# Eight experts in a row: longer turns in the first product's loop, a loop in the second product, and the opening moved ahead of the hand-synchronised section

## The chip, the cores and the metric

One core of one Trainium2 chip. The time is the device time of one launch in microseconds (us); lower is better. The profile shows five engines, named as in its rows: PE (TensorE's matmuls, and PEld for its weight loads), DVE (VectorE), ACT (ScalarE), POOL (GpSimd) and SP (SyncE). An engine's sequencer reads its instructions in order; rows of instructions that the sequencer does alone (address arithmetic, branches, waits) carry a q behind the engine's name, as in PEldq.

## The reference

Eight experts, each with 256 tokens of 512 numbers; every expert has its own two weight matrices and biases.

```python
n_experts, capacity, hidden, expert_hidden = 8, 256, 512, 2048
h = np.matmul(x, w1) + b1[:, np.newaxis, :]
h = np.maximum(h, 0)
return (np.matmul(h, w2) + b2[:, np.newaxis, :]).astype(np.float32)
```

All inputs and the output are fp32 in HBM.

## The kernel before

**Tiling.** The weights, and x from expert 2 on, are turned into fp16 on their way by GpSimd's DMAs. x is transposed on VectorE in blocks of 32 by 32 (`transposes`, L166 to L187), so that the first product gives h transposed: 16 columns of 128 hidden units, each with 256 tokens, each the sum of four matmuls (L299) in one of four PSUM banks `ph`. ScalarE takes a column out of its bank, adds b1 and applies relu (L234) into `hT`. The second product takes, for each half of 128 tokens (`tb`), one matmul that lays b2 down as ones times b2 (L320) and 16 matmuls of 512 columns (L323), in two groups of eight (`lo` 0 and 8), since the last two experts' second weights come in two halves. VectorE evicts token half 0 and ScalarE token half 1 (`evict`, L189 to L203). The experts' outputs are stored in groups of four and two by GpSimd (`flush`), the last two singly by SyncE.

**Stages.** TensorE runs a loop of 11 stages (L288). In stage s it does the first product of expert s (if s is under 8) and then the second product of expert s - 3 (if s is at least 3; `LAG` is 3). So stages 0 to 2 hold a first product only, stages 3 to 7 both, stages 8 to 10 a second product only. The loop is a loop on the chip: its instructions stand once in the program, and addresses are worked out in registers by TensorE's sequencer ahead of each matmul. The first product is itself a loop on the chip (L295), four turns of four columns (`NPH` is 4). The second product is written out: 34 matmuls, one behind the other.

**What sets the order.** Everything after the two `tile_critical` lines (L88) is synchronised by hand with semaphores; the instructions of each engine run in the order written.

- POOL: the DMAs of w1, w2 and x in one queue (L144 to L154), with three buffers for each kind of weights. A load waits for the product that last used its buffer (L122, L130).
- SP: waits for each weight to land and then counts `s_go` up (`go`, L245); `s_go` is what TensorE waits for ahead of each first product (L293) and of each group of eight of the second (L315).
- PE: beside `s_go` it waits for the transposes (`s_xT`, L294), and for a free bank of `po` ahead of each token half (`s_free`, L319). A column waits until its `ph` bank is free: `s_credit` starts at 4, ScalarE adds one for each column taken out, each column's first matmul waits for its number in the turn (L307), and at the end of a turn 4 are taken off (L309).
- DVE: the opening (cast of x of expert 0, its transposes, cast of x of expert 1, transposes of b1), and then in each stage the transposes for the next expert and the eviction of half 0.
- ACT: 16 columns of a stage, then the eviction of half 1.

The opening (memset, a warming activation, b1's load, the two x loads, casts and transposes) stands inside the section, with semaphores of its own (`s_ones`, `s_self`, `s_b1`).

Of the kernel before, what the change touches and what calls it, by code (L numbers as in the profile page):

```python
# [10 lines left out]
def kernel(  # L11
# [12 lines left out]
    nc = tc.nc  # L24
# [4 lines left out]
    E, T, H = x.shape  # L29
# [44 lines left out]
    for first, n in GROUPS.items():  # L74
# [5 lines left out]
    po = ctx.enter_context(nc.psum_tensor("po", [P, 2 * nTB * H], fp32))  # L80

    s_last = sem("last_stores")
    nc.vector.sem_inc(s_last, 16 * len(HALVED))

    section = ctx.enter_context(ExitStack())
    section.enter_context(tc.tile_critical(  # L88
        sync_engine=mybir.EngineType.SP, no_gpsimd_drain=True))


    landed = {}

    def load(engine, key, **kw):
        landed[key] = sem(f"d_{key}")
        engine.dma_start(**kw).then_inc(landed[key], 16)  # L96

    s_ones = sem("ones")
    s_self = sem("dve_self")
    s_b1 = sem("b1T")  # L100
    s_xT = sem("xT")
    s_ph = sem("ph")
    s_credit = sem("ph_free")
    s_po = [sem(f"po{tb}") for tb in range(nTB)]
    s_free = [sem(f"po{tb}_free") for tb in range(nTB)]
    s_out = [sem(f"out{tb}") for tb in range(nTB)]
    s_go = sem("weights")


    for e in range(2):  # L110
        load(nc.sync, f"x{e}", out=x32[e][:], in_=x[e].rearrange("(p tb) h -> p tb h", tb=nTB))


    def load_x(first):
# [12 lines left out]

    def load_w2(e):
        if e >= NW:
            nc.gpsimd.wait_ge(s_po[1], e - NW + 1)  # L130
        dst = w2_sb[:, e % NW * nJ * H : (e % NW + 1) * nJ * H].rearrange("p (j h) -> p j h", j=nJ)
        src = w2[e].rearrange("(p j) h -> p j h", j=nJ)
        size = half if e in HALVED else nJ
        for lo in range(0, nJ, size):
            load(nc.gpsimd, f"w2_{e}_{lo}", out=dst[:, lo : lo + size], in_=src[:, lo : lo + size])
# [22 lines left out]


    nc.vector.sem_inc(s_last, -16 * len(HALVED))  # L160
    nc.vector.memset(ones1[:], 1.0).then_inc(s_ones, 1)  # L161
    nc.scalar.wait_ge(s_ones, 1)
    nc.scalar.activation(out=warm[:], in_=ones1[:], func=relu)  # L163
    load(nc.scalar, "b1", out=b1_rows[:], in_=b1.rearrange("e (b i) -> (e b) i", b=nB))

    def transposes(e):  # L166
        t, p0, R = x16[e]
        n = R // nTB
        if e >= 2:
            first = max(f for f in X_LOADS if f <= e)  # L170
            nc.vector.wait_ge(landed[f"x{first}"], 16)
            nc.vector.wait_ge(s_ph, nJ * (e - 1))
        mine = xT[:, e % 2 * nKC * T : (e % 2 + 1) * nKC * T].rearrange("p (kc t) -> p kc t", kc=nKC)
        last = None
        for g in range(T // R // B):
            src = t[p0 + B * g : p0 + B * (g + 1)]
            for b in range(nB):
                block = src[:, :, b * (H // nB) : (b + 1) * (H // nB)].rearrange(
                    "p (n tb) (i kc) -> p tb kc n i", tb=nTB, kc=nKC)
                dst = mine[b * B : (b + 1) * B].rearrange(  # L180
                    "p kc (tb g i n) -> p tb g kc n i", tb=nTB, i=B, n=n)
                if n == 1:
                    last = nc.vector.transpose(out=dst[:, :, g, :, 0, :], in_=block[:, :, :, 0, :])  # L183
                    continue
                for tb in range(nTB):
                    last = nc.vector.transpose(out=dst[:, tb, g], in_=block[:, tb])  # L186
        last.then_inc(s_xT, 1)  # L187

    def evict(e, tb):  # L189
        engine = nc.scalar if tb else nc.vector  # L190
        copy = nc.scalar.copy if tb else nc.vector.tensor_copy
        first, n = group_of.get(e, (e, 1))
        rows = P // n
        at = (e - first) * rows
        engine.wait_ge(s_po[tb], e + 1)
        for k in range(n):
            bank = (e % 2 * nTB + tb) * H
            last = copy(out=results[e][at : at + rows, k * nTB + tb, :],  # L198
                        in_=po[k * rows : (k + 1) * rows, bank : bank + H])
        last.then_inc(s_out[tb], 1)  # L200
        if e + 2 < E:
            engine.wait_ge(s_out[tb], e + 1)
            engine.sem_inc(s_free[tb], 1)  # L203

    for e in range(2):
        nc.vector.wait_ge(landed[f"x{e}"], 16)
        nc.vector.tensor_copy(out=x16[e][0][:], in_=x32[e][:]).then_inc(s_self, 1)  # L207
        nc.vector.wait_ge(s_self, e + 1)
        if e == 0:
            transposes(e)  # L210
    nc.vector.wait_ge(landed["b1"], 16)
    for b in range(nB):
        last = nc.vector.transpose(  # L213
            out=b1T[b * B : (b + 1) * B, nB - 1 - b : nB - 1 - b + nJ * B],
            in_=b1_rows[:].rearrange("r (i j) -> r j i", j=nJ),
        )
    last.then_inc(s_b1, 1)
    for s in range(E + LAG):
        if s + 1 < E:
            transposes(s + 1)  # L220
        if s >= LAG:
            evict(s - LAG, 0)

    nc.scalar.wait_ge(s_b1, 1)
    for s in range(E + LAG):
        if s < E:
            split = group_of.get(s, (s, 1))[1]
            if s > LAG:
                nc.scalar.wait_ge(s_po[1], s - LAG)
            for j in range(nJ):  # L230
                at = (s % (LAG + 1) * nJ + j) * T
                bias_at = j * B + s * nB + nB - 1
                nc.scalar.wait_ge(s_ph, nJ * s + j + 1)
                nc.scalar.activation(  # L234
                    out=hT[:, at : at + T].rearrange("p (tb k i) -> p tb k i", tb=nTB, k=split),
                    in_=ph[:, j % NPH, 0:T].rearrange("p (tb i k) -> p tb k i", tb=nTB, k=split),
                    func=relu,
                    bias=b1T[:, bias_at : bias_at + 1],
                    scale=1.0,
                ).then_inc(s_credit, 1)  # L240
        if s >= LAG:
            evict(s - LAG, 1)


    def go(key, n=1):  # L245
        nc.sync.wait_ge(landed[key], 16)
        nc.sync.sem_inc(s_go, n)
# [5 lines left out]
    for s in range(E + LAG):  # L253
        if s == 0:
            nc.sync.wait_ge(landed["b2"], 16)
        if s < E:
            go(f"w1_{s}")
        e = s - LAG
        if e >= 0 and e not in HALVED:
            go(f"w2_{e}_0", 2)  # L260
        elif e == E - 2:
            go(f"w2_{e}_0")
            go(f"w2_{e}_{half}")
        elif e == E - 1:
            go(f"w2_{e}_0")
            for tb in range(nTB):
                nc.sync.wait_ge(s_out[tb], e)
            store(E - 2, 0, P, nc.sync)
            go(f"w2_{e}_{half}")
# [5 lines left out]


    nc.tensor.sem_inc(s_credit, NPH)
    for tb in range(nTB):
        nc.tensor.sem_inc(s_free[tb], 2)
    nc.tensor.wait_ge(s_ones, 1)  # L280

    def take(s, n=1):
        nc.tensor.wait_ge(s, n).then_inc(s, -n)  # L283
# [4 lines left out]
    with nc.Fori(0, E + LAG, 1, engines=[PE]) as s:  # L288
        nc.tensor.wait_ge(s_credit, NPH)
        w_at = at(s % NW * (nKC * M), (NW - 1) * nKC * M)  # L290
        with nc.tensor.If(s < E):
            x_at = at((s & 1) * (nKC * T), nKC * T)
            take(s_go)  # L293
            take(s_xT)  # L294
            with nc.Fori(w_at, w_at + nJ, NPH, engines=[PE]) as w_from:  # L295
                w_from = w_from.with_bounds(min_val=0, max_val=(NW - 1) * nKC * M + nJ - NPH)
                for j in range(NPH):
                    for kc in range(nKC):
                        last = nc.tensor.matmul(  # L299
                            ph[:, j, 0:T],  # L300
                            w1_sb[:, bass.ds(w_from + (kc * M + j), P, nJ)],
                            xT[:, bass.ds(x_at + kc * T, T)],
                            start=(kc == 0),
                            stop=(kc == nKC - 1),
                        )
                        if kc == 0:
                            last.wait_op(s_credit, j + 1, "sem-ge")  # L307
                    last.then_inc(s_ph, 1)
                nc.tensor.sem_inc(s_credit, -NPH)  # L309
        with nc.tensor.If(s >= LAG):  # L310
            b_at = at((s - LAG) * H, (E - 1) * H)
            h_at = at(((s + 1) & LAG) * (nJ * T), LAG * nJ * T)
            p_at = at(((s + 1) & 1) * (nTB * H), nTB * H)
            for lo in range(0, nJ, half):
                take(s_go)  # L315
                for tb in range(nTB):
                    bank = po[:, bass.ds(p_at + tb * H, H)]
                    if lo == 0:
                        take(s_free[tb])  # L319
                        nc.tensor.matmul(bank, ones1[:], b2_sb[:, bass.ds(b_at, H)],  # L320
                                         start=True, stop=False)
                    for j in range(lo, lo + half):
                        last = nc.tensor.matmul(  # L323
                            bank,
                            hT[:, bass.ds(h_at + (j * T + tb * P), P)],
                            w2_sb[:, bass.ds(w_at + j * H, H)],
                            start=False,
                            stop=(j == nJ - 1),
                        )
                    if lo:  # L330
                        last.then_inc(s_po[tb], 1)

    section.close()
    nc.sync.wait_ge(s_last, 16 * len(HALVED))


# [28 lines left out]
```

## Time and profile before

| what | value |
|---|---|
| median of 3 runs | 184.51 us (184.13 to 184.54) |
| the profiled execution's own time | 184.6 us |
| its span, first to last instruction | 182.7 us |
| PE busy, matmuls | 137.7 us, 784 matmuls |
| DVE busy | 87.5 us |
| ACT busy | 72.8 us |
| read from HBM | 71.39 MB, 414 GB/s over the span |
| mean granted clock of TensorE | 0.981 of full speed |

How to read it: a timeline row holds the start and length in us, the engine, the line in the kernel, the operation, what it writes and reads, how many instructions the row joins, and in brackets the idle time of the engine ahead of it and what ended it. `PEq L283` means that TensorE's own sequencer, at a wait of L283, ended it. A group's row holds the busy time, the mean of one instruction in ns, and the idle time ahead of its instructions with its causes. A row of one line in a window holds the count, minimum, median and maximum in ns, and the start of the first and of the last in us. Matmuls are pipelined: each one's length is longer than the distance to the next.

### The profile page before, as it was taken

Reading aid. Unit: us, or ns where it says so; the run is one execution under the profiler, and the core shown is the slowest. Engines: PE = TensorE matmul, PEld = TensorE weight load, DVE = VectorE, ACT = ScalarE, POOL = GpSimd, SP = SyncE. Lnnn points to the kernel's source line nnn. Section 1 sums busy time; section 2 is a strip of 40 time slices with the busy share of each in tenths; the row PEclk is TensorE's granted clock in tenths of the full one; section 3 lists DMA queues with packets and bytes.
Section 4 is the critical chain, followed back from the end, with each engine's and each line's share of the span. In section 5 each row is a group of like instructions: output and inputs, shape, how many; then the busy total and the mean of one; then the engine's idle time right before and its main releaser. Section 6 shows DMA issues by size and latency. Waiting matters only on the chain. (4 is left out here: it accounts for less than half of the span.)

```text
span 182.7 us, 3079 instructions
## 1 busy us (share of the span) xinstructions
PE 137.7 (75%) x784; PEld 92.5 (51%) x784; DVE 87.5 (48%) x125; ACT 72.8 (40%) x152; POOL 12.5 (7%) x27
## 2 busy tenths in 40 slices
PE   0003886977958779777996779786996879999990
PEld 0003784865847654576355644585465834344340
DVE  0999938409300497998059931997060003030110
ACT  3001663774655740577019530775038610220101
POOL 6000003001020010100010000100020000301000
PEclk9999998898899999999999999999999999999999
DMA  5989998999999998999999999999899989999972
GB/s 192 278 179 228 230 226 183 222 230 228 212 196 219 237 215 190 230 226 222 194 219 226 230 208 197 230 226 222 187 226 226 230 185 219 213 217 231 423 294 115
DMA packets 3826, 40.46 MB, mean 221 GB/s; under 512 B 448, under 2 KB 464, under 8 KB 1136
## 3 DMA queue, kind: packets, MB, share of 16 engines
q0 software_dynamic: 3200, 38.28, 95.0%
q1 hardware_dynamic: 576, 2.10, 3.0%
q10 hardware_dynamic: 48, 0.07, 0.1%
q14 instruction: 2, 0.02, 0.0%
HBM read 71.39 MB, written 4.19 MB: 414 GB/s over the span
## 5 line engine op out<-in xcount | busy, mean ns | idle before, releaser
L299 PE MATMUL ph<-xT,w_sb 128*128 x512 | 75.7, 305 | 35.8 <-PEq L283 21.9
L299 PEld LDWEIGHTS ph<-xT,w_sb 128*128 x512 | 66.9, 146 | 45.0 <-issue 22.4
L234 ACT ACTIVATE hT<-ph,b1T 128x256 f16<-128x256 f32 x128 | 58.5, 475 | 42.9 <-PE ph L299 39.5
L186 DVE STREAM_TRANSPOSE xT<-x 32x256 f16<-32x256 f16 (+1 forms) x64 | 52.8, 893 | 25.9 <-DMA x<-in_x_dram 18.1
L323 PE MATMUL po<-w_sb,hT 128*128 x256 | 58.0, 380 | 0.1
L323 PEld LDWEIGHTS po<-w_sb,hT 128*128 x256 | 24.1, 97 | 30.2 <-issue 4.1
L198 DVE COPY out<-po 32x512 f32<-32x512 f32 (+1 forms) x20 | 13.7, 687 | 46.0 <-PE po L323 45.8
L198 ACT COPY out<-po 32x512 f32<-32x512 f32 (+1 forms) x20 | 11.6, 579 | 48.7 <-PE po L323 48.5
L96 POOL DMA_DIRECT2D w_sb<-in_w_dram x18 | 9.7, 544 | 144.9 <-PE po L323 74.8
L183 DVE STREAM_TRANSPOSE xT<-x 32x256 f16<-32x256 f16 x32 | 14.0, 436 | 0.5
L320 PE MATMUL po<-b_sb,ones 1*128 x16 | 6.1, 380 | 4.9 <-PEq L283 4.9
L198 DVE COPY x<-po 128x512 f32<-128x512 f32 x2 | 1.4, 692 | 13.4 <-PE po L323 13.4
L320 PEld LDWEIGHTS po<-b_sb,ones 1*128 1x128 f16 x16 | 1.4, 90 | 10.3 <-issue 10.3
L198 ACT COPY x<-po 128x512 f32<-128x512 f32 x2 | 1.2, 587 | 13.8 <-PE po L323 13.8
L213 DVE STREAM_TRANSPOSE b1T<-b_rows 32x512 f32<-32x512 f32 x4 | 4.1, 1024 | 0.1
L207 DVE CAST x<-x 128x1024 f16<-128x1024 f32 x2 | 1.4, 694 | 2.9 <-DMA x<-in_x_dram 2.9
L163 ACT ACT_TABLE_LOAD x1 | 1.3, 1283 | 0.9 <-SPq L88 0.9
L96 POOL DMA_DIRECT2D out_dram<-out x2 | 1.1, 542 | 7.7 <-ACT out L198 7.7
L96 POOL DMA_DIRECT2D x<-in_x_dram x2 | 1.1, 550 | 0.0
L161 DVE MEMSET ones<- 1x128 f16 x1 | 0.2, 165 | 1.2 <-SPq L88 1.2
L96 POOL DMA_DIRECT2D b_sb<-in_b_dram x1 | 0.5, 509 | 0.0
L163 ACT ACTIVATE warm<-ones 1x128 f16<-1x128 f16 x1 | 0.3, 308 | 0.0
(4 smaller groups left out, 0.4 us busy)
## 6 DMA issues: line engine op xcount, KB each, us to landing
w_sb<-in_w_dram POOLq DMA_DIRECT2D x14, 2048.0 KB, 35.7
w_sb<-in_w_dram POOLq DMA_DIRECT2D x4, 1024.0 KB, 16.1
out_dram<-out POOLq DMA_DIRECT2D x1, 2048.0 KB, 17.9
x<-in_x_dram SPq DMA_DIRECT2D x2, 512.0 KB, 5.1
x<-in_x_dram POOLq DMA_DIRECT2D x1, 1024.0 KB, 33.0
out_dram<-out POOLq DMA_DIRECT2D x1, 1024.0 KB, 13.1
out_dram<-x SPq DMA_DIRECT2D x2, 512.0 KB, 4.7
x<-in_x_dram POOLq DMA_DIRECT2D x1, 512.0 KB, 24.8
```

The lines of the kernel that those rows point to most:

```text
L96: engine.dma_start(**kw).then_inc(landed[key], 16)
L161: nc.vector.memset(ones1[:], 1.0).then_inc(s_ones, 1)
L163: nc.scalar.activation(out=warm[:], in_=ones1[:], func=relu)
L183: last = nc.vector.transpose(out=dst[:, :, g, :, 0, :], in_=block[:, :, :, 0, :])
L186: last = nc.vector.transpose(out=dst[:, tb, g], in_=block[:, tb])
L198: last = copy(out=results[e][at : at + rows, k * nTB + tb, :], in_=po[k * rows : (k + 1) * rows, bank : bank + H])
L207: nc.vector.tensor_copy(out=x16[e][0][:], in_=x32[e][:]).then_inc(s_self, 1)
L213: last = nc.vector.transpose(out=b1T[b * B : (b + 1) * B, nB - 1 - b : nB - 1 - b + nJ * B], in_=b1_rows[:].rearrange("r (i j) -> r j i", ...
L234: nc.scalar.activation(out=hT[:, at : at + T].rearrange("p (tb k i) -> p tb k i", tb=nTB, k=split), in_=ph[:, j % NPH, 0:T].rearrange("p ( ...
L299: last = nc.tensor.matmul(ph[:, j, 0:T], w1_sb[:, bass.ds(w_from + (kc * M + j), P, nJ)], xT[:, bass.ds(x_at + kc * T, T)], start=(kc == 0 ...
L320: nc.tensor.matmul(bank, ones1[:], b2_sb[:, bass.ds(b_at, H)], start=True, stop=False)
L323: last = nc.tensor.matmul(bank, hT[:, bass.ds(h_at + (j * T + tb * P), P)], w2_sb[:, bass.ds(w_at + j * H, H)], start=False, stop=(j == nJ ...
```

## The change

Four parts:

- **First product:** the inner loop makes two turns of eight columns instead of four of four. The four `ph` banks are used twice in a turn, so a column's number in the turn goes up to 8 and 8 credits are taken off at a turn's end.
- **Second product:** the two token halves are a loop on the chip of two turns, once for each group of eight matmuls, instead of being written out. The bank's offset is worked out from the loop's counter. One semaphore `s_po` counts both halves (2 e + tb + 1) instead of one for each.
- **Gating by SyncE:** TensorE no longer waits for the transposes nor for free `po` banks. SyncE waits for `s_xT` before it releases a w1, and from the third expert on for the evictions of the expert two back before it releases a w2.
- **Opening:** the memset, the warming activation, the loads of b1 and of x of experts 0 and 1, the casts, expert 0's transposes and those of b1 stand ahead of the section. The section's beginning waits, on PE, ACT, SP and DVE, until they are done; POOL's queue of loads stands ahead of that wait. The wait for the last stores is an instruction of SyncE behind the section.

```diff
-    for e in range(2):
-        load(nc.sync, f"x{e}", out=x32[e][:], in_=x[e].rearrange("(p tb) h -> p tb h", tb=nTB))
...
+    nc.vector.memset(ones1[:], 1.0)
+    tc.keep_in_program_order(nc.scalar.activation(out=warm[:], in_=ones1[:], func=relu))
+    tc.keep_in_program_order(nc.scalar.dma_start(
+        out=b1_rows[:], in_=b1.rearrange("e (b i) -> (e b) i", b=nB)))
+    for e in range(2):
+        nc.sync.dma_start(out=x32[e][:], in_=x[e].rearrange("(p tb) h -> p tb h", tb=nTB))
+    for e in range(2):
+        nc.vector.tensor_copy(out=x16[e][0][:], in_=x32[e][:])
+        if e == 0:
+            transposes(e)
+    for b in range(nB):
+        nc.vector.transpose(
+            out=b1T[b * B : (b + 1) * B, nB - 1 - b : nB - 1 - b + nJ * B],
+            in_=b1_rows[:].rearrange("r (i j) -> r j i", j=nJ),
+        )
+
+    section = ctx.enter_context(ExitStack())
+    by_hand = section.enter_context(tc.tile_critical(
+        sync_engine=mybir.EngineType.SP, no_gpsimd_drain=True))
...
+    nc.vector.sem_inc(s_xT, 1)
...
-        engine.wait_ge(s_po[tb], e + 1)
+        engine.wait_ge(s_po, nTB * e + tb + 1)
...
-        if e + 2 < E:
-            engine.wait_ge(s_out[tb], e + 1)
-            engine.sem_inc(s_free[tb], 1)
...
         if s < E:
+            nc.sync.wait_ge(s_xT, s + 1)
             go(f"w1_{s}")
         e = s - LAG
+        if e >= 2:
+            for tb in range(nTB):
+                nc.sync.wait_ge(s_out[tb], e - 1)
...
             take(s_go)
-            take(s_xT)
-            with nc.Fori(w_at, w_at + nJ, NPH, engines=[PE]) as w_from:
...
-                for j in range(NPH):
+            with nc.Fori(w_at, w_at + nJ, half, engines=[PE]) as w_from:
...
+                for j in range(half):
...
-                            ph[:, j, 0:T],
+                            ph[:, j % NPH, 0:T],
...
-                nc.tensor.sem_inc(s_credit, -NPH)
+                nc.tensor.sem_inc(s_credit, -half)
...
                 take(s_go)
-                for tb in range(nTB):
-                    bank = po[:, bass.ds(p_at + tb * H, H)]
+                with nc.Fori(h_at, h_at + T, P, engines=[PE]) as h_from:
+                    h_from = h_from.with_bounds(min_val=0, max_val=LAG * nJ * T + T - P)
+                    o_at = at(p_at + (h_from & P) * (H // P), (2 * nTB - 1) * H)
+                    bank = po[:, bass.ds(o_at, H)]
                     if lo == 0:
-                        take(s_free[tb])
...
-                            hT[:, bass.ds(h_at + (j * T + tb * P), P)],
+                            hT[:, bass.ds(h_from + j * T, P)],
...
-                        last.then_inc(s_po[tb], 1)
+                        last.then_inc(s_po, 1)
...
-    nc.sync.wait_ge(s_last, 16 * len(HALVED))
+    landing = nc.sync.nop().wait_op(s_last, 16 * len(HALVED), "sem-ge")
```

In the changed program a turn of the second product's first group holds, on TensorE's sequencer, a two-register step, three ALU steps (one a multiplication), two more steps, the bias matmul, eight pairs of a two-address step and a matmul, a two-register step and a branch; a turn of the second group has one step less ahead of its matmuls and no bias. In the kernel before, token half 1's matmuls each had a one-address step.

## The prediction

> **What bounds the kernel now.** I read the chain of work that ended last and the groups first, then the timeline of TensorE, then the waits of SyncE for the weights, and last the single lines of TensorE's sequencer.
>
> ```profile
> PE 17%; ACT 0%; issue 0%
> PE po L323 16%; PE po L320 1%; ACT x L198 0%
> ...
> L299 PE MATMUL ph<-xT,w_sb 128*128 x512 | 75.7, 305 | 35.8 <-PEq L283 21.9
> ...
> L323 PE MATMUL po<-w_sb,hT 128*128 x256 | 58.0, 380 | 0.1
> ```
>
> The chain is TensorE alone. The second product (L323) runs almost without a gap (0.1 us idle in 58.0). The first (L299) loses 35.8 us, 16.6 of it before its first matmul.
>
> ```profile
> 42.28 8.11 PE L299 MATMUL ph<-xT,w_sb 128*128 x48 [1.78 <-PEq L283]
> ...
> 55.04 2.35 PE L299 MATMUL ph<-xT,w_sb 128*128 x16 [1.74 <-PEq L283]
> ...
> 63.73 2.35 PE L299 MATMUL ph<-xT,w_sb 128*128 x16 [0.53 <-ACT hT L234]
> 67.06 0.37 PE L320 MATMUL po<-b_sb,ones 1*128 x1 [0.98 <-PEq L283]
> ...
> 74.79 1.91 PE L299 MATMUL ph<-xT,w_sb 128*128 x16
> 78.06 2.32 PE L299 MATMUL ph<-xT,w_sb 128*128 x16 [1.36 <-ACT hT L234]
> 80.92 2.36 PE L299 MATMUL ph<-xT,w_sb 128*128 x16 [0.54 <-ACT hT L234]
> 83.80 2.35 PE L299 MATMUL ph<-xT,w_sb 128*128 x16 [0.52 <-ACT hT L234]
> 87.13 0.37 PE L320 MATMUL po<-b_sb,ones 1*128 x1 [0.98 <-PEq L283]
> ...
> 135.00 1.91 PE L299 MATMUL ph<-xT,w_sb 128*128 x16
> ```
>
> Stages 4 to 7 repeat every 20.07 us (67.06 to 87.13). Stages without a second product take 12.76 us (42.28 to 55.04). After stage 7 only second products are left:
>
> ```profile
> 155.17 0.38 PE L320 MATMUL po<-b_sb,ones 1*128 x1
> ...
> 162.93 0.38 PE L320 MATMUL po<-b_sb,ones 1*128 x1
> ...
> 170.68 0.38 PE L320 MATMUL po<-b_sb,ones 1*128 x1
> ...
> 173.15 5.35 PE L323 MATMUL po<-w_sb,hT 128*128 x24
> ```
>
> They repeat every 7.76 us and end at 178.50. The weights arrive earlier. These rows are SyncE's releases, three windows of the one line:
>
> ```profile
> L247 SPq EVENT_SEMAPHORE  x5: 17/17/28, 15.7 to 57.2; - x5
> L247 SPq EVENT_SEMAPHORE  x7: 17/17/17, 71.8 to 129.9; - x7
> L247 SPq EVENT_SEMAPHORE  x5: 17/17/17, 139.6 to 163.8; - x5
> ```
>
> From 71.8 to 129.9 six steps bring three experts, 19.4 us each. The cover is 3.0 us at stage 4 (71.8 against 74.79), 5.1 at stage 7 (129.9 against 135.00) and 6.9 for the last expert's first half (163.8 against 170.68). So TensorE's stream is the bound, with the DMAs close behind.
>
> **What paces TensorE's stream.** The sequencer, lines of it in short windows (columns: count, min/median/max ns, first to last start):
>
> ```profile
> L309 PEldq EVENT_SEMAPHORE  x1: 51/51/51, 80.1 to 80.1; - x1
> L295 PEldq FUSED_REGOPS  x1: 42/42/42, 80.2 to 80.2; - x1
> L295 PEldq COMPARE_BRANCH  x1: 218/218/218, 80.3 to 80.3; - x1
> L295 PEldq MOVE  x1: 29/29/29, 80.6 to 80.6; - x1
> L299 PEldq ALU_OP  x1: 36/36/36, 80.7 to 80.7; - x1
> L299 PEldq FUSED_REGOPS  x2: 74/76/79, 80.8 to 80.9; - x2
> L295 PEldq COMPARE_BRANCH  x1: 83/83/83, 86.1 to 86.1; - x1
> L323 PEldq FUSED_REGOPS  x8: 74/74/79, 157.2 to 158.2; - x8
> L323 PEldq FUSED_REGOPS  x8: 46/46/51, 158.4 to 159.3; - x8
> L288 PEldq ALU_OP  x2: 36/36/36, 152.6 to 159.4; - x2
> L323 PEldq FUSED_REGOPS  x33: 46/57/98, 154.2 to 159.3; - x33
> ```
>
> Each matmul needs one address step. With two new addresses it takes 74 ns and the next follows after 0.155 us, with one 46 ns and 0.126 us (eight from 157.2 to 158.2, eight from 158.4 to 159.3). A turn's foot and head, the first five rows, take 0.7 us (80.1 to 80.8): the 0.52 to 0.54 us gaps above are the sequencer's, though the view names ACT. Their durations sum to 0.38, so each step costs its row plus about 0.06: ALU 0.095, move 0.09, a two-register step 0.10, a semaphore wait 0.11 to 0.15 (I take 0.15), a branch 0.275 taken (218) and 0.14 not taken (83). One pass over a last stage is 6.8 us (152.6 to 159.4), under TensorE's 7.76, so today the sequencer runs ahead there.
>
> **The change, part by part.**
>
> *Eight columns a turn.* Two of three turn ends go: 0.7 each, and four two-address steps become one-address ones (4 x 0.03): 0.83 each. Stages 0 to 3 gain 1.66. From stage 4 on the first boundary lies under a wait that stays:
>
> ```profile
> 74.99 2.35 ACT L198 COPY out<-po 32x512 f32<-32x512 f32 x4 [8.40 <-PE po L323]
> 77.53 2.34 ACT L234 ACTIVATE hT<-ph,b1T 128x256 f16<-128x256 f32 x6 [0.19 <-ACT out L198]
> ```
>
> ScalarE evicts the previous expert until 77.34, its first activation frees a bank near 78.0, and TensorE resumes at 78.06. So one boundary is gained there, 0.83. ScalarE keeps up: its backlog clears at 0.39 us a column (2.34 for 6) against 0.5 for four matmuls.
>
> *Second product as a loop over token halves.* Twice per expert a loop of two turns; weights' addresses are computed again in each, so all steps are two-address (0.155). A first-half turn: head of a two-register step, three ALU, two more steps and the bias matmul, 0.64; eight steps 1.24; 0.05 for the remainder of the stage number by three (98 against 57), now taken in every turn; foot 0.10 and a branch: 2.31 taken, 2.17 not. A second-half turn has one step less in its head and no bias: 2.18 and 2.05. With two waits for weights (0.30), two ALU, a step and a move (0.38) that is 9.4 us an expert. TensorE needs 1.94 a turn (7.76/4): now the sequencer is slower, and every turn shows. A pass in the tail adds 0.85 (ALU, move, two branches taken, one not): 10.25 instead of 7.76. Not shown before: the multiply as ALU step, nothing extra (36) up to the remainder step's 98, so 0 to 0.06 a turn; I take nothing, as ALU rows all read 36.
>
> The Trainium skill, "Advanced Engine Details and Errata", section "Control Flow Timing", gives about 108 ns for a compare-and-branch. The rows show 218 and 83. By the page's figure the 28 turns counted below would be about 1.2 us cheaper (an estimate), which would give 189.0; the rows decide.
>
> *Waits moved to SyncE.* TensorE's three waits a stage, for two free banks and the transposes, go; the sums here are without them. SyncE now waits for the transposes ahead of each first-product weight, and for evictions ahead of the second's; weights behind them in its queue wait too. The eviction asked for is two experts back, over at least one pass of 7.76 before the release is needed, so that pass hides it; if it came late, TensorE would stop by the lateness.
>
> *Opening outside the section.* TensorE, ScalarE and SyncE now enter behind all of VectorE's opening:
>
> ```profile
> 12.97 4.14 DVE L213 STREAM_TRANSPOSE b1T<-b_rows 32x512 f32<-32x512 f32 x4
> ...
> 62.07 9.96 DVE L186 STREAM_TRANSPOSE xT<-x 32x512 f16<-32x512 f16 x8 [14.64 <-DMA x<-in_x_dram]
> ...
> 16.62 5.31 PE L299 MATMUL ph<-xT,w_sb 128*128 x32 [16.62 <-PEq L283]
> ```
>
> It ends at 17.11; with VectorE's two semaphore steps (0.3) and the 0.9 from SyncE's release (15.7) to the first matmul (16.62), the first matmul comes at 18.3: 1.7 later. Bounds: 0.5 (17.11 itself) to 2.6 (one more such 0.9 hop). POOL's loads stand ahead of the wait and start as before.
>
> **The sum.** Stages 0 to 3 gain 6.6, lose 1.7: stage 3's first product ends 4.9 earlier, 66.1 (63.73 + 2.35) to 61.2. Then come 0.4 of loop end, a branch (0.14), 9.4, and 0.6 of ALU, move and branches to the wait for the next weights: 71.7, or 71.5 as the sequencer is 0.2 ahead of the last end. There something else is late: expert 4's transposes wait for x (landed at 62.07) and end at 72.03 whatever TensorE does. Through SyncE (0.9 as at the start, less a wait: 0.75) stage 4 starts at 72.8, 2.0 earlier than 74.79; 2.9 of the gain is lost. A period is then 64 matmuls 8.3 (8 x 0.155, 56 x 0.126), boundary 0.7, loop end and branch 0.5, second product 9.4, entry 1.1 (two ALU, two moves, two branches, a wait, a remainder step), and 0.1, as a measured turn (2.88, 80.92 to 83.80) is 0.05 over its steps: 20.1. TensorE's last matmul now trails the sequencer by 0.46, since its eight take 0.216 each ((5.35 - 0.38)/23) against 0.155; ScalarE's eviction, and so column 5, is later by that, 0.3 of it uncovered: add 0.3 from stage 5 on. Stage 5: 92.9; 6: 113.3; 7: 133.7 (135.00 before). Expert 5's bias matmul follows after 0.3 + 8.25 + 0.7 + 0.5 + 9.4 + 1.9 (0.85 and the head of a second product): 154.7 (155.17). Then 10.25 twice: 175.2 (170.68). To the last end it is 10.25 less that 1.9 and a foot, 8.1, and the trailing 0.46 and a matmul's 0.38: 184.1 instead of 178.5. That is 5.6 us more. Behind it stand the same eviction and store (the profiled run takes 184.6 us, span 182.7): 184.6 + 5.6 = **190.2**. The median of the runs is 184.51, 0.1 lower, so I keep 190.2. A measurement of this kernel can tell about 0.3% (0.55 us) from no change.
>
> **Rivals.**
>
> *Faster: the turn ends hide behind the matmuls*, as in the old tail. For: 58.0 us of L323 with 0.1 idle. Against: 0.7 at each L295 turn. If a turn costs no more than TensorE's 1.94, the DMAs bound next: stage 7 would start at 129.9 + 0.75 = 130.65, then 11.5 to expert 4's bias (12.34, 74.79 to 87.13, less 0.83) and four times 7.76: 173.2, or 179.3 in all. It decides below 2.0 us a turn: 5.6 us over the 28 turns of stages 4 to 10 is 0.2 off the mean 2.18. 8%.
>
> *Slower still: the halved clock.*
>
> ```profile
> 43.90:47.20 3.30, 3.17 (x16) 2.29 (x15) 3.25 (x9) 1.72 (x5) 0.00 (x0) 0.50 1.13 241
> ...
> 47.40:178.00 130.60, 111.91 (x630) 71.00 (x629) 55.27 (x55) 53.01 (x112) 6.89 (x13) 1.00 1.01 227
> ```
>
> The granted clock (third column from the end) was 0.50 from 43.9, behind the 1.78 us gap that ends at 42.28, and 1.00 after 47.4, though one gap of 1.74 (to 55.04) lies there. In the changed kernel the gap between the products grows from 0.98 to about 1.2, with smaller ones (0.35) after each turn. A half-clock stretch lets 16 matmuls of the first product through (the row's x16) instead of 27 (3.4/0.126), 1.4 us, of which about 1 stays lost after catching up; three of them: 193.2. 20%. The Trainium skill, "TensorE: Matmul & The Clock Gate", Part 1, lets the clock fall only after an idle window of about 3.4 us; by that rule it stays at 190.2, but the 0.50 above followed a shorter gap.
>
> *The early gain does not last to stage 4.* Its cover is short: 0.5 us between 71.5 and the release at 72.05. Entry at its upper bound (0.9 more) and two half-clock stretches of 1 us, which today's turn ends partly hide, put stage 4 at 72.8 + 2.4 = 75.2: 192.6. 12%.
>
> **The numbers.** Forecast 60% (187 to 193: 28 turns by 0.1 are 2.8 either way), faster rival 8%, clock 20%, lost gain 12%. The range 186.0 to 194.5 leaves out the faster rival and the ends of the others, together under 2 in 10. The faster rival's weight splits into 6% faster by over 0.3% and 2% within it; the forecast's low tail adds 1% within. Faster 0.06, same 0.03, slower 0.91.
>
> **What would show it.** First-product rows of 32 matmuls with one gap of 0.5 us between them. Stage 4's first matmul near 72.8, behind VectorE. Bias matmuls 10.2 us apart in the tail, with idle of about 0.35 us ahead of each turn put to the sequencer. The second product's group with several us idle instead of 0.1. Bias matmuls still 7.8 apart would prove the sum wrong, and a half clock after 75 us the second rival right.

## The result, and the profile after

The changed kernel takes **192.28 us** (median of 4 runs, 191.77 to 192.67), the kernel before 184.40 beside it: a ratio of 1.0427, 95% interval 1.0394 to 1.046. The forecast was 190.2 (range 186.0 to 194.5). The profiled run took 192.59, span 190.8.

The page of the changed kernel: the chain that ended last, by engine and by line, and two rows of the groups (busy time, mean ns | idle time before them).

```profile
PE 17%; issue 3%; ACT 2%; SPq 0%
PE po L314 16%; PE po L311 2%; ACT out L204 1%; ACT x L204 1%; SPq L241 0%; SPq L237 0%; SPq L261 0%
...
L314 PE MATMUL po<-w_sb,hT 128*128 x256 | 60.8, 380 | 5.8 <-issue 5.8
...
L311 PE MATMUL po<-b_sb,ones 1*128 x16 | 6.1, 382 | 13.4 <-issue 8.8
```

The chain is still TensorE, now with 3% of "issue", time in which it waits for nothing that the profile shows. The second product (L314) was idle for 0.1 us before and is for 5.8 now; its bias matmuls (L311) for 13.4. The timeline of TensorE shows where, in the first stages, in stage 4 and in the tail:

```profile
18.28 9.86 PE L289 MATMUL ph<-xT,w_sb 128*128 x64 [18.28 <-PEq L274]
29.78 4.40 PE L289 MATMUL ph<-xT,w_sb 128*128 x32 [1.64 <-PEq L274]
34.72 4.40 PE L289 MATMUL ph<-xT,w_sb 128*128 x32 [0.54 <-ACT hT L223]
...
51.72 9.50 PE L289 MATMUL ph<-xT,w_sb 128*128 x64 [1.63 <-PEq L274]
62.65 0.38 PE L311 MATMUL po<-b_sb,ones 1*128 x1 [1.43 <-issue]
...
72.53 4.44 PE L289 MATMUL ph<-xT,w_sb 128*128 x32 [0.73 <-PEq L274]
77.50 4.40 PE L289 MATMUL ph<-xT,w_sb 128*128 x32 [0.54 <-ACT hT L223]
83.31 0.38 PE L311 MATMUL po<-b_sb,ones 1*128 x1 [1.41 <-issue]
83.62 1.90 PE L314 MATMUL po<-w_sb,hT 128*128 x8
85.71 0.38 PE L311 MATMUL po<-b_sb,ones 1*128 x1 [0.19 <-issue]
86.03 1.90 PE L314 MATMUL po<-w_sb,hT 128*128 x8
88.31 1.90 PE L314 MATMUL po<-w_sb,hT 128*128 x8 [0.38 <-issue]
90.55 1.90 PE L314 MATMUL po<-w_sb,hT 128*128 x8 [0.35 <-issue]
93.17 4.46 PE L289 MATMUL ph<-xT,w_sb 128*128 x32 [0.72 <-PEq L274]
...
113.84 4.49 PE L289 MATMUL ph<-xT,w_sb 128*128 x32 [0.67 <-PEq L274]
...
156.09 0.38 PE L311 MATMUL po<-b_sb,ones 1*128 x1 [1.52 <-SPq L237]
...
166.77 0.38 PE L311 MATMUL po<-b_sb,ones 1*128 x1 [1.54 <-SPq L237]
...
177.49 0.38 PE L311 MATMUL po<-b_sb,ones 1*128 x1 [1.52 <-SPq L237]
...
184.72 1.90 PE L314 MATMUL po<-w_sb,hT 128*128 x8 [0.33 <-issue]
```

Read it against the rows of before. A first product is now two rows of 32 with one gap of 0.54 (in stages 0, 2 and 3 one row of 64, in which the gap does not show), and the stages without a second product repeat every 10.97 us (40.75, one row left out above, to 51.72) instead of 12.76: that is the gain. Every turn of the second product has a gap of 0.2 to 0.4 ahead of it, every pass 1.4 to 1.5: that is the loss. In the tail a pass takes 10.68 (156.09 to 166.77) instead of 7.76. Stage 4 starts 2.3 us earlier than before, stage 7 0.5 earlier, expert 5's bias matmul 0.9 later, the last matmul ends at 186.62 instead of 178.50.

One label has to be doubted. Ahead of the last three passes the idle time is put down to SyncE (`SPq L237`), 4.6 us in all. The sequencer's own rows ahead of 156.09 (count, min/median/max ns, first to last start) say otherwise:

```profile
L306 PEldq ALU_OP  x2: 36/36/36, 155.0 to 155.1; - x2
...
L311 PEldq ALU_OP  x3: 32/36/36, 155.5 to 155.7; - x3
L311 PEldq FUSED_REGOPS  x2: 47/95/143, 155.8 to 156.0; - x2
...
L274 PEldq EVENT_SEMAPHORE  x1: 51/51/51, 154.9 to 154.9; - x1
```

It was past its wait for weights (L274) at 154.9 and worked out addresses without a pause until 156.0. SyncE's wait of 2081 ns that begins at 153.7 ends at 155.8 and stands in the middle of that: it releases expert 6, not expert 5. A label is the last event ahead of an instruction, which need not be its cause; two experiments below test this one.

### The profile page after: what moved, and what is told of

Its sections match the earlier page's. It is cut to its first block, busy times and chain, and to the rows that moved or that the text cites. A ratio compares the mean times of both kernels' runs of the same rounds, so it can differ in the third digit from the quotient of the medians.

```text
span 190.8 us, 3193 instructions
## 1 busy us (share of the span) xinstructions
PE 138.7 (73%) x784; PEld 92.5 (48%) x784; DVE 87.4 (46%) x125; ACT 72.3 (38%) x152; POOL 12.5 (7%) x27
## 5 line engine op out<-in xcount | busy, mean ns | idle before, releaser
L289 PE MATMUL ph<-xT,w_sb 128*128 x512 | 72.8, 305 | 28.8 <-PEq L274 26.0
L314 PE MATMUL po<-w_sb,hT 128*128 x256 | 60.8, 380 | 5.8 <-issue 5.8
L314 PEld LDWEIGHTS po<-w_sb,hT 128*128 x256 | 24.3, 97 | 38.1 <-issue 17.2
L311 PE MATMUL po<-b_sb,ones 1*128 x16 | 6.1, 382 | 13.4 <-issue 8.8
L311 PEld LDWEIGHTS po<-b_sb,ones 1*128 1x128 f16 x16 | 1.5, 91 | 19.7 <-issue 19.7
```

Of the source, the lines that this page charges most:

```text
L289: last = nc.tensor.matmul(ph[:, j % NPH, 0:T], w1_sb[:, bass.ds(w_from + (kc * M + j), P, nJ)], xT[:, bass.ds(x_at + kc * T, T)], start=(k ...
L314: last = nc.tensor.matmul(bank, hT[:, bass.ds(h_from + j * T, P)], w2_sb[:, bass.ds(w_at + j * H, H)], start=False, stop=(j == nJ - 1),)
```

## The experiments

Theory: TensorE's sequencer now paces the second product, at the heads and feet of its turns; the other three parts of the change cost nothing or gain. Rivals: **A**, SyncE's wait for evictions stands ahead of the tail's passes; **B**, the opening's 1.7 us last to the end; **C**, the two-address steps are the cost, not the turns.

| kernel | median, us | ratio to before, 95% interval |
|---|---|---|
| SyncE's waits alone | 182.24 | 0.9882 (0.9862 to 0.9901) |
| eight columns alone | 183.59 | 0.9951 (0.9931 to 0.9971) |
| eight columns and SyncE's waits | 183.51 | 0.9947 (0.9929 to 0.9964) |
| loop over token halves alone | 206.01 | 1.1167 (1.1144 to 1.1189) |
| changed, second product written out | 183.36 | 0.9941 (0.9922 to 0.9961) |
| changed, opening inside | 192.06 | 1.0406 (1.0385 to 1.0427) |
| changed, four columns a turn | 204.46 | 1.1085 (1.1066 to 1.1103) |
| changed, tighter wait for evictions | 195.46 | 1.0605 (1.056 to 1.0649) |
| changed, two turns of 17 matmuls | 183.53 | 0.9952 (0.9935 to 0.9968) |
| written out, first group store left out | 179.56 | 0.9753 (0.9727 to 0.9779) |
| before, first group store left out | 184.26 | 0.9998 (0.9989 to 1.0008) |
| written out, landing waits behind the section | 181.93 | 0.9865 (0.9848 to 0.9881) |

### The second product written out again, and the loop alone

```diff
-                with nc.Fori(h_at, h_at + T, P, engines=[PE]) as h_from:
...
+                for tb in range(nTB):
+                    bank = po[:, bass.ds(p_at + tb * H, H)]
```

> The changed kernel with the second product written out again for both token halves; eight columns a turn, SyncE's waits and the opening outside the section stay. Theory (the loop over token halves is the only part that loses, since TensorE's sequencer then needs more than TensorE's 1.94 us a turn): stages 0 to 3 as in the changed kernel, stage 4 starts about 0.7 us behind SyncE's release at 71.4, so 72.1; then the weights' 19.4 us an expert pace it, stage 7 near 130.3, expert 4's bias matmul 141.8, four passes of 7.76: last matmul 172.9, time 179.0 us. Rival A (SyncE's wait for evictions is what stands ahead of the bias matmuls of experts 5 to 7, 1.5 us each, as the view of waits says): those three waits stay, 183.6 us. Rival B (the opening's 1.7 us lasts to the end): 180.7 us.

Measured: 183.36. The loop costs 8.9 us of the changed kernel's time, and without it the change would be a gain of 0.6%. By its time alone this run would fit rival A (183.6) and not the theory (179.0); the rows decide. The waits of 1.5 us are gone from the last two passes: the bias matmuls of experts 5 to 7 come at 150.17, 157.99 and 165.75, the last two with no idle time ahead. SyncE waits there as in the changed kernel, so this speaks against A. TensorE did what was expected (its last matmul ends at 173.74 for 172.9, and 12.9 ahead of the changed kernel's 186.62), but the run ended 4.4 later than expected. What took that is settled further down.

The loop put into the kernel before, with the two bank waits ahead of it:

> The kernel before with the loop over token halves alone (both bank waits of an expert stand ahead of its loop). Theory: no gain ahead of stage 4, so nothing hides there; a stage's period grows by the 1.4 us that the loop costs in the changed kernel (20.67 against 19.24 for one boundary) and 0.15 for a bank wait that now stands ahead: stage 4 at 76.4, stage 7 at 141.3; the tail's passes take about 10.9 instead of 7.76. Last matmul about 196.4, time 202 us (200 to 204). Rival A (the loop costs little and SyncE's waits are what loses): 184.5 to 187 us.

Measured: 206.01, 4 us over the middle of the expectation. SyncE waits for no eviction here, so the loss is the loop's and not A's. Two rows of the bias matmuls, experts 0 and 1:

```profile
67.46 0.38 PE L324 MATMUL po<-b_sb,ones 1*128 x1 [1.71 <-issue]
...
90.13 0.47 PE L324 MATMUL po<-b_sb,ones 1*128 x1 [1.72 <-issue]
```

A period is 22.67, against 20.07 before and 21.65 expected: in a stage the loop costs 2.6 us, not 1.6. Most of the missing 1.0 is explained at the four-column run.

### The parts that gain: eight columns, SyncE's waits

```diff
-            with nc.Fori(w_at, w_at + nJ, NPH, engines=[PE]) as w_from:
+            with nc.Fori(w_at, w_at + nJ, half, engines=[PE]) as w_from:
```

> The kernel before with eight columns a turn alone. Theory: 6.6 us earlier at the end of stage 3's first product, then stage 4 waits for the transposes and SyncE's release (71.8) and starts at 72.7; periods 19.24 of TensorE's own against 19.4 of the weights, stage 7 at 130.8: last matmul 173.4, time 179.5 us. Rival (turn ends are worth only what the first four stages show, and the rest is hidden by ScalarE's evictions): 182.5 us. If the loop over token halves were harmless, this would be no more than 1 us faster than the changed kernel's other parts make it, and the changed kernel would not be slower at all.

Measured: 183.59, 0.7 faster than before and not 5; the rival's 182.5 is the nearer number. Yet its last matmul ends at 173.99, close to the 173.4 expected and 4.5 ahead of before: as with the second product written out, TensorE gains and the run does not.

```diff
+            nc.sync.wait_ge(s_xT, s + 1)
...
-            take(s_xT)
...
-                        take(s_free[tb])
```

> The kernel before with SyncE's waits in place of TensorE's three, alone. Theory: 0.15 us less of TensorE's sequencer per wait that stood in a gap, one per first product and one per second (the other is run ahead of): stage 4 at 73.9 instead of 74.79, stage 7 at 132.2 to 133.2, last matmul 176.4, time 182.4 us; no idle ahead of the bias matmuls in the tail. Rival A (SyncE's release behind the eviction is late): bias matmuls in the tail 1.5 us late, three times, 187 us.

Measured: 182.24, as the theory has it (182.4). Taking three waits out of TensorE's sequencer is a gain of 2.1 by itself: a stage's period falls from 20.07 to 19.74 (66.17 to 85.91, the bias matmuls of experts 0 and 1), and the tail keeps its 7.76 with SyncE waiting for evictions, which speaks against A once more.

### The opening back inside, and a tighter wait

First the changed kernel with the fourth part of its diff undone:

> The changed kernel with the opening put back into the hand-synchronised section; eight columns, the loop and SyncE's waits stay. Theory (the opening's delay is absorbed at stage 4, which waits for expert 4's transposes): first matmul 16.6 instead of 18.28, stage 3's second product done 1.7 earlier, but stage 4 starts no earlier than 72.0 instead of 72.53, as SyncE's release stays at 71.4: 0.4 to 0.5 faster than the changed kernel, 191.8 us. Rival B (the delay lasts): 1.7 faster, 190.6 us.

Measured: 192.06 against 192.28, within what can be told apart. The first matmul came at 16.79, 1.5 earlier, and stage 4 at 72.71, no earlier than the changed kernel's 72.53: TensorE, ahead by then, stands idle for 2.69 us until expert 4's transposes are done (71.98) and SyncE has released the weight. So an earlier opening gains nothing there. B falls.

```diff
-        if e >= 2:
+        if e >= 1:
             for tb in range(nTB):
-                nc.sync.wait_ge(s_out[tb], e - 1)
+                nc.sync.wait_ge(s_out[tb], e)
```

> The changed kernel with SyncE's wait for evictions one expert tighter (the expert just before, not the one two back). Theory (in the changed kernel that wait is over long before TensorE asks, and the 1.5 us ahead of the tail's bias matmuls are TensorE's sequencer): now the wait does decide in the tail, a release 1.2 us behind the last matmul of the expert before plus 0.3 of SyncE and 0.7 to 1.0 to the first matmul, so gaps of 2.2 to 2.5 instead of 1.52 at experts 5 and 6 and about 1.8 at expert 7; nothing in stages 4 to 7: 2 us slower than the changed kernel, 194.3 us. Rival A (the changed kernel already waits there for the expert just before): the same time as the changed kernel, 192.3 us.

Measured: 195.46 (194.59 to 196.28), 3.2 us slower than the changed kernel where 2 were expected; its profiled run took 195.13. The bias matmuls of experts 5 to 7 in this kernel:

```profile
157.12 0.38 PE L311 MATMUL po<-b_sb,ones 1*128 x1 [2.48 <-issue]
...
168.71 0.38 PE L311 MATMUL po<-b_sb,ones 1*128 x1 [2.44 <-issue]
...
180.02 0.38 PE L311 MATMUL po<-b_sb,ones 1*128 x1 [1.90 <-SPq L237]
```

and the sequencer's waits for weights, first to last start:

```profile
L274 PEldq EVENT_SEMAPHORE  x6: 51/51/51, 155.9 to 184.0; - x6
```

Here TensorE passes the first of these waits at 155.9 and not at 154.9. The gaps are 2.48, 2.44 and 1.90 instead of 1.52 to 1.54, 2.2 us in all. The two profiled runs differ by 2.5 (195.13 against 192.59), and about 0.2 of that goes with the lower clock behind 168.71 that the last section shows (that pass takes 11.31 instead of 10.72, and 0.38 of the difference is the gap behind it); what the median has beyond (3.2) is not explained. When SyncE's wait does decide, two of the three gaps are called "issue"; when it does not, as in the changed kernel, they bear SyncE's name. With this A is out.

### Heads and feet, or steps

```diff
-            for lo in range(0, nJ, half):
-                take(s_go)
+            if True:
+                take(s_go, 2)
                 with nc.Fori(h_at, h_at + T, P, engines=[PE]) as h_from:
...
-                    for j in range(lo, lo + half):
+                    for j in range(nJ):
```

> The changed kernel with two turns of 17 matmuls an expert in place of four of 9 and 8: the loop over token halves takes all sixteen columns in a turn (both releases of an expert's weights are asked for at its start, and SyncE gives the last expert's second half ahead of a store). Each step still has two addresses. Theory (the turns' heads and feet cost, not the steps): a turn is 16 steps of 0.155 and about 1.15 around them, 3.65, against TensorE's 3.68; a pass about 8.5 instead of 10.7; stage 4 at 72.1, stage 7 near 130.5, last matmul 175, time 181 us. Rival C (the two-address steps are the cost, not the turns): a pass of 10 us or more, 189 us or more.

Measured: 183.53. The steps still have two addresses each, and yet it is 8.75 us faster than the changed kernel, 0.5% faster than before. The page's groups of this kernel:

```profile
L314 PE MATMUL po<-w_sb,hT 128*128 x256 | 59.7, 388 | 0.0
L311 PE MATMUL po<-b_sb,ones 1*128 x16 | 6.1, 383 | 10.8 <-issue 10.8
```

Within a pass nothing idles; what is left is the entry of each pass, 1.4. C falls: sixteen steps of 0.155 fit under TensorE's 3.68, and only a head and foot for every nine or eight matmuls does not. (A pass also has one wait for weights and one entry into a loop fewer here, so the run weighs these together with two heads and feet.) The 2.5 over the expectation are passes of 9.2 instead of 8.5 (140.87 to 150.09), as a sequencer that only keeps step with TensorE hides none of a pass's entry (this is argued, not tested); a wait for both halves of expert 6's weights, whose second was released at 158.6 (a gap of 1.91 ahead of 159.81); and the half clock told of in the last section.

### Four columns a turn, the loop kept

The changed kernel with the first part of its diff undone:

> The changed kernel with four columns a turn as before; loop, SyncE's waits and opening outside stay. Theory: without the 6.6 us gained ahead of stage 4 the loop and the opening's 1.7 us have nothing to hide behind: stage 4 at 74.79 + 1.7 + 1.4 - 0.9 = 77.0, periods of 20.67 + 0.83 = 21.5, stage 7 at 141.5, last matmul 194.4, time 200.5 us. Rival (eight columns bring nothing once the sequencer paces the second product): under 195 us.

Measured: 204.46, 4 us over the expectation, the second time by that much. One stage of this kernel:

```profile
78.50 2.36 PE L289 MATMUL ph<-xT,w_sb 128*128 x16 [0.72 <-PEq L274]
81.39 2.35 PE L289 MATMUL ph<-xT,w_sb 128*128 x16 [0.53 <-ACT hT L223]
84.27 2.35 PE L289 MATMUL ph<-xT,w_sb 128*128 x16 [0.53 <-ACT hT L223]
```

The first boundary costs 0.53 here, not the 1.36 of the kernel before. There TensorE began a stage at once behind its last matmul and then waited at column 4 (the fifth, counting from 0) for ScalarE, which was still evicting. With the loop TensorE begins 0.72 late, ScalarE is done by then, and no wait remains at column 4. So all boundaries are plain turn ends, and eight columns save two of them in every stage: the period is 22.22 (68.68 to 90.90) against the changed kernel's 20.66 (62.65 to 83.31). The loop costs more than I took, and the eight columns give more back.

### Where the gain of the written-out kernel went

TensorE ends at 173.74 there and the span at 181.5. SyncE's waits in that kernel from 150 on:

```profile
SPq L265 <- ACT x L204: 4.6, 1, 4.6
SPq L268 <- DMA out_dram<-out: 3.7, 1, 3.7
```

SyncE waits 3.7 us for a group store to land, until 178.5 (L268); in the changed kernel that line's wait was over when SyncE came to it. The DMA rows of both, in 40 slices of the span, first the kernel with the second product written out:

```profile
DMA  6999999999999999999999999999999999999992
GB/s 211 265 220 190 228 228 206 204 231 228 200 209 213 235 209 209 231 217 209 209 231 217 209 209 231 217 206 213 231 217 202 217 208 218 209 222 182 438 402 88
```

and the changed kernel:

```profile
DMA  6999999999999999999999999999999999996202
GB/s 228 226 220 222 220 220 220 218 220 220 211 199 230 209 210 209 220 220 220 220 220 220 220 216 220 220 210 220 216 210 201 210 220 216 196 400 289 110 0 110
```

In the written-out kernel the DMA engines are at nine tenths or more from the second slice to the last but one: the stores, 4 MB in all, stand behind all the weights. In the three kernels that store everything, keep these waits in the section and whose TensorE ends 4.3 to 4.8 us ahead of before, SyncE saw the group stores land at 178.5 (this one), 178.6 (eight columns alone) and 178.9 (eight columns and SyncE's waits). Two runs leave the store of experts 0 to 3 out, one of the written-out kernel, one of the kernel before:

```diff
-    for first in GROUPS:
-        flush(first)
+    flush(4)
```

> The changed kernel with the second product written out, and without the store of experts 0 to 3 (2 MB, left out of the output). The same kernel with that store had its last matmul end at 173.74, 4.8 before the kernel before, and was only 0.9 faster. Theory (the stores stand behind the last weights in the DMA engines, which are full to the end, so the end is theirs): the other store lands about 5 us earlier (2 MB at the 400 GB/s of the last slices), and the end follows TensorE: 173.7 + 4.2 to the span's end, time 179.8 us (179.3 to 180.3). Rival (something in the closing steps that has nothing to do with the stores): no change, 183.4 us.

> The kernel before without the store of experts 0 to 3 (2 MB, left out of the output). Theory (there TensorE's last eviction and its store end the run, and the group stores land ahead of them): no change, 184.3 us. Rival (the DMAs bound the kernel before too): 2 us or more faster.

Measured: 179.56 and 184.26, both as the theory has it. In the first of them SyncE no longer has to wait for a group store; its last long wait is for ScalarE's last eviction (4.9 us, L264). In the kernel before the stores are done in time and cost nothing; with TensorE 4.8 us ahead, they and what comes behind them are the end. The next run puts eight columns and SyncE's waits together into the kernel before:

> The kernel before with eight columns a turn and SyncE's waits, nothing else. Theory (TensorE's stream is then 4 to 5 us ahead of the stores, which end the run as with eight columns alone): last matmul near 173.3, time 183.4 us, no faster than SyncE's waits alone (182.24). Rival (the gains of the two parts add up): 181.5 us or less.

Measured: 183.51. The gains of the two parts do not add up, and together they are slower than SyncE's waits alone, 182.24. The reason is in the closing. SyncE waits 3.7 us for a group store there too and passes that line at 178.9; with its waits alone it passed it at 177.3 without waiting. In the kernels that have these waits in the section the span ends 3.0 or 3.1 us behind that line (before: 179.6 and 182.7; SyncE's waits alone: 177.3 and 180.4; both parts: 178.9 and 181.9; written out: 178.5 and 181.5; changed: 187.7 and 190.8). GpSimd's closing lies in these 3 us and is as long, 1929 ns, in each of the five:

```profile
L351 POOLq DRAIN  x3: 45/83/1929, 178.8 to 181.2; - x3
```

That is the written-out kernel, from 178.8. (Why the stores land by 177.3 with SyncE's waits alone, where the second of them is issued at 162.53, and only at 178.5 in the written-out kernel, where it is issued at 159.85, is open.) So the waits for the group stores were moved behind the section:

```diff
-    for first in GROUPS:
-        nc.sync.wait_ge(landed[f"out{first}"], 16)
...
-    landing = nc.sync.nop().wait_op(s_last, 16 * len(HALVED), "sem-ge")
+    for s, n in [(s_last, 16 * len(HALVED))] + [(landed[f"out{first}"], 16) for first in GROUPS]:
+        landing = nc.sync.nop().wait_op(s, n, "sem-ge")
```

> The changed kernel with the second product written out, and SyncE's waits for the two group stores moved behind the hand-synchronised section, so that GpSimd's 1.93 us of closing run beside the stores. Theory: the end is then the landing of the last expert's store (179.56 there) and 0.9, span 180.4, time 182.2 us, against 183.36. Rival (GpSimd's closing itself waits until its stores have landed): 183.4 us.

```profile
L357 POOLq DRAIN  x3: 45/83/3718, 175.4 to 180.2; - x3
```

Measured: 181.93. The closing starts at 175.4 and lies beside the stores. It takes longer there (3718 ns) and ends at 179.1, still ahead of the last store, whose landing SyncE waits for until 179.4. This is the fastest that computes everything, 0.9865 of before; SyncE's waits alone, 0.9882, cannot be told apart from it.

## Why the prediction was right, and where its terms were not

| event | forecast | measured | difference added |
|---|---|---|---|
| first matmul | 18.3 | 18.28 | 0.0 |
| stage 3's first product ends | 61.2 | 61.22 | 0.0 |
| stage 4 | 72.8 | 72.53 | -0.3 |
| stage 7 | 133.7 | 134.54 | +1.1 |
| expert 5's bias matmul | 154.7 | 156.09 | +0.6 |
| expert 7's bias matmul | 175.2 | 177.49 | +0.9 |
| last matmul ends | 184.1 | 186.62 | +0.2 |

**The mechanism held, except at stage 4.** The first products gain 6.5 us, the opening costs 1.7, and from stage 3 on the loop paces TensorE's second product, as forecast. But stage 4 was to start "behind VectorE", whose transposes for expert 4 were to end at 72.03, with TensorE ready at 71.5. The changed kernel's rows are these, the transposes, SyncE's release and TensorE's wait for it:

```profile
61.60 9.82 DVE L122 STREAM_TRANSPOSE xT<-x 32x512 f16<-32x512 f16 x8 [15.93 <-DMA x<-in_x_dram]
...
L237 SPq EVENT_SEMAPHORE  x1: 28/28/28, 71.4 to 71.4; - x1
...
L274 PEldq EVENT_SEMAPHORE  x1: 51/51/51, 71.9 to 71.9; - x1
```

The transposes end at 71.42, as their x landed 0.5 earlier, and TensorE's sequencer comes to its wait 0.5 us after the release. It goes on at once: from there to the first matmul take 0.6 us, as at stage 5 (92.5 to 93.17). So nothing was lost at the transposes here. Between the end of stage 3's first product and stage 4 lie 11.3 us (61.22 to 72.53) where 8.7 lay before (66.08 to 74.79): these 2.6 us are the loop's, in stage 3 itself. That stage 4 came within 0.3 of its forecast is luck: the sequencer was 0.4 later than forecast, and the wait of 0.55 for the transposes did not come. The transposes do decide where TensorE is earlier, as with the opening inside and with the second product written out (idle for 2.69 and 2.51 us ahead of stage 4).

**The turn's head was too small.** The prediction priced the head's register steps from rows of 42 ns, and the one with the remainder from 98. The changed kernel's sequencer, a first-half turn and then a second-half turn of expert 1:

```profile
L311 PEldq FUSED_REGOPS  x1: 148/148/148, 83.0 to 83.0; - x1
...
L314 PEldq FUSED_REGOPS  x1: 125/125/125, 83.3 to 83.3; - x1
...
L314 PEldq FUSED_REGOPS  x1: 177/177/177, 87.9 to 87.9; - x1
```

The step behind a head's three ALU steps takes 148 or 177, the first weight step behind a bias matmul 125. The kernel before had shown steps of that size, outside the windows that the prediction read: one of 119 at the entry of the first product's loop (L295, at 73.2). A turn is about 0.1 longer than forecast: from one bias matmul to the next it takes 2.40 (83.31 to 85.71) instead of 2.31. Four turns make the 0.43 by which the first tail pass is over 10.25. For the seven passes from stage 4 on that is 3.0: this is the term that was mis-sized, and the prediction had put its uncertainty there (28 turns by 0.1). The sum was 2.5 short and not 3.0 because smaller errors of both signs stand beside it: the 0.3 at stage 4, and two that are told of under ScalarE's wait.

**The multiply and the branches were priced right.** ALU rows of L311 read 32 to 36, so the multiply costs nothing extra. A branch at a turn's end was 218 taken and 83 not; the new loop's rows read 220 and 78.

**ScalarE's wait at column 4 went.** "From stage 4 on the first boundary lies under a wait that stays" is wrong beside the loop, as the four-column run shows: two boundaries are gained. The sum did not use it, as it counts the sequencer's steps with one boundary. It did use "add 0.3 from stage 5 on", for the same wait, and that did not come. A period took 20.67 (93.17 to 113.84) where 20.1 + 0.3 was forecast; without the 0.3 and with the turns at their real price it would be 20.53, so 0.14 a period came from steps that I had too cheap and did not trace further. Over the stages the two come to -0.6 and +0.4 and nearly cancel, which is luck as well.

**SyncE's waits cost nothing**, as forecast, for the reason given: expert 6's release at 155.8 comes 9.8 us before TensorE asks for it (165.6). The run with the tighter wait shows from where they would cost. Alone they are a gain of 2.1, which the prediction did not name as a term.

**The faster rival had the wrong price.** Its 179.3 took the weights as the next bound and forgot the stores that stand behind them in the same DMA engines, and the closing behind the stores. The written-out kernel, which is that case, took 183.36, and the run without one store 179.56. With the right price the rival would have ended 0.6% below before, not 2.8%. The other rivals did not come. The clock was granted at 0.50 in two stretches of stages 2 and 3, and at 1.00 from 62 to 187; one window of that is the last row here:

```profile
42.30:45.70 3.40, 3.40 (x18) 2.73 (x17) 3.31 (x9) 2.10 (x5) 0.00 (x0) 0.50 1.08 231
52.50:55.90 3.40, 3.40 (x19) 2.68 (x18) 0.00 (x0) 1.90 (x5) 0.00 (x0) 0.50 0.90 190
...
73.00:155.00 82.00, 67.86 (x391) 45.32 (x389) 41.19 (x40) 36.62 (x79) 2.78 (x6) 1.00 1.01 215
```

The first products of these stages, 9.34 and 9.50, are hardly longer than one at full clock with its turn end (4.40 + 0.54 + 4.40 = 9.34): the turn's end does not show, as the sequencer could run ahead meanwhile. Of the four runs the one with a mean clock of 1.000 took 191.96, within the range of the other three (0.970 to 0.979).

## What to carry to other kernels

A loop on the chip costs its engine's sequencer a head and a foot for every turn (here about 1.1 us of 2.4), which is free only while the turn holds more of the engine's work than the sequencer's: count both, and make the turn longer (17 matmuls instead of 9) before writing it out. Before pricing a gain, ask what ends second: here 4.8 us of TensorE's time were worth 0.9, as stores stood behind the last loads in DMA engines that were already full. An idle time's label names the last event before an instruction; look at the sequencer's rows, and tighten the suspected wait, before believing it.

## What the runs showed of the hardware

- **The clock after short gaps.** The granted clock fell behind gaps of 1.6 to 2.4 us, but not behind each. In the run with the tighter wait the gap of 2.48 was followed by matmuls at full pace, the gap of 2.44 by this window (the granted clock is the third column from the end):

```profile
168.80:172.20 3.40, 3.40 (x10) 1.04 (x9) 0.00 (x0) 0.00 (x0) 0.00 (x0) 0.65 0.99 424
```

  With two turns a gap of 1.91 ahead of 159.81 was followed by this one:

```profile
160.10:163.50 3.40, 3.40 (x9) 1.21 (x9) 0.00 (x0) 0.00 (x0) 0.13 (x1) 0.51 1.06 222
```

  A row of 16 matmuls took 5.30 there instead of 3.63. The Trainium skill, "TensorE: Matmul & The Clock Gate", Part 1, lets the clock fall after an idle window of about 3.4 us, and also tells of a kernel with short idle times between groups of matmuls whose clock went up and down. No gap of 3.4 us stands ahead of any of these stretches, so here the rows decide. The length of a gap alone doesn't tell when it falls, and the runs don't settle what else does.
- **Branches.** 208 to 237 ns taken, 68 to 83 not, in the rows of TensorE's sequencer in both kernels. The Trainium skill, "Advanced Engine Details and Errata", section "Control Flow Timing", has one figure, about 108 ns; it is half of the one and above the other.
- **Long register steps.** In the head of a turn single steps take 125, 148 and 177 ns, where an address step takes 46 or 74. In the kernel before the longest ahead of a second product's matmul is 101, but the entries of the first product's loop have one of 119 to 143 each. What makes a step long isn't shown.
- **GpSimd's closing** took 1.93 us where it stood behind the landing of the group stores and 3.72 where it lay beside them. Whether it waits for them in part isn't shown.
